# A planner's clock counts TensorE's products by form: a two-layer hybrid trunk on one core

## The chip, the cores and the metric

The kernel runs on one NeuronCore of a Trainium2 chip. The metric is the device time of one execution in microseconds (us), taken as the median over several runs.

## The reference

The program computes a two-layer trunk over 256 context tokens and 256 latent tokens of width 1024, all in float32. Each layer modulates and normalises its tokens, projects them, and runs three mixers side by side (a gated MLP over chunks, a windowed attention with eight heads, a state-space scan), joins them with one output projection, and then applies a feed-forward part. In layer 0 that part is one dense SwiGLU of width 2816 over all 512 tokens. In layer 1 it is a mixture of eight SwiGLU experts of the same width, of which each of the 256 latent tokens takes two:

```
logits = h @ w_r
top_v, top_i = top_k(logits, 2);  gates = softmax(top_v)
out = sum over e of combine[:, e] * ((silu(h @ wg[e]) * (h @ wu[e])) @ wd[e])
x = x + mod[5] * out
```

## The kernel before, in words

**Stages.** Before the experts come the modulation, both mixers and the dense feed-forward (function `phase_a`), then the routing. The experts are the function `experts`. Weights stream from HBM in pieces of 1 MB (two gate-and-up pieces and one down piece for each of the 11 chunks of 256 hidden columns of an expert, so 264 pieces) into a ring of raw buffers `wraw`, which grows to 12 during the experts.

**Places and rounds.** Routed experts are sorted by their number of tokens into eight places with 160, 128, 128, 64, 64, 64, 32 and 32 slots (place 0 is computed as 128 slots and a rest of 32, called NE). Places 0, 1 and 2 are wide: their weights are split into a high part `whi` (ScalarE, L275) and a low part `wlo` (VectorE, L276), each in two halves of 1024 columns, and TensorE makes three fp32r products from the parts, with 512 columns each. Narrow places (64 or 32 slots) use the raw float32 weights with the token block as the stationary operand, two or four products side by side in strips of the array (`tiled`, L1561, for 64 slots and for the down products; `tiled_up`, L1570, for 32 slots). One round of `experts` is one chunk of a wide place (tile `gu`), the down products of the last chunk (`py`), and chunks of narrow places that are dealt out over the rounds; after the narrow up products ScalarE copies them out as `mid`, TensorE turns them (`mTx`, `mT`), and ScalarE and VectorE make the activations `silx`, `mh` and `ml`. A round of place 0 holds its two raw tiles longer, since the rest NE reads them too (`gux`, then `pyx`). The order of places is: four rounds of a 32-slot place alone, 11 rounds of place 1, 11 of place 0, 11 of place 2, two rounds of a 32-slot place alone.

**The planner's clock.** While the program is written out, an object `Order` keeps a clock `clk` in microseconds that stands for TensorE's progress. Every product (`mm`, L368) and every transpose (`tp`, L381) adds a price to it. Side chains (gathering an expert's tokens, `gather`; the transposed one-hot tables, `onehot`; adding an expert's result to the output, `finish`) are generators that yield a delay; `poll` lets a chain take its next step at the next yield of the main program at which `clk` has reached the time that it asked for.

```
f = 1 if (l.dtype == F32R and n >= 256) else 4
self.o.clk += f * max(n, 64) * 0.000422 + 0.002
```

The class `Weights` models the transfers on the same clock: a piece lands at `max(queue + PIECE, clk + LANDS)` (L243), a half split takes `SPLIT` (L277), and a split is laid ahead of its need when `clk` is past the landing and past the last planned split less half a `SPLIT` (`_due`, L288, asked when a product group gives a buffer back). `get` (L311) moves `clk` forward to the planned landing or split of the piece that is needed next.

**What the clock orders.** In the experts TensorE and ScalarE execute in the order in which the program is written (`MSB = "pa"`); VectorE and SyncE, and all engines before the experts (`MSA = ""`), are put in order by the framework's scheduler, for which the written order is the rank. The order of the weight pieces is a fixed list.

Of the kernel before, what the change touches and what calls it, by code (L numbers as in the profile page):

```python
# [10 lines left out]
F32R = mybir.dt.float32r  # L11
# [198 lines left out]
def until(cond):  # L210
    while not cond():
        yield 0.5
# [128 lines left out]
class Net:  # L341
# [26 lines left out]
    def mm(self, out, l, r, start, stop):  # L368
        n = 1
        for x in r.shape[1:]:  # L370
            n *= x
        f = 1 if (l.dtype == F32R and n >= 256) else 4
        self.o.clk += f * max(n, 64) * 0.000422 + 0.002
        self.nc.tensor.matmul(out, l, r, start=start, stop=stop)  # L374

    def warm(self, src, n):
# [2 lines left out]
            self.nc.tensor.matmul(self.idle[:, :256], self.c("ident"), src, start=True, stop=True)  # L379

    def tp(self, out, src, n=P):  # L381
        self.o.clk += 0.11
        ident = self.c("ident")
        self.nc.tensor.transpose(out, src, ident if n == P else ident[0:n, 0:n])  # L384

# [60 lines left out]
    def mods(self, l, ns):  # L446

        ps = self.bulk("modp")
        for i, n in enumerate(ns):
            if l == 0 and 0 < n < 4:  # L450
                self.o.clk += self.SU
                yield
# [1064 lines left out]
        self.ohT[p] = ohT  # L1517

    SU = 4.0
    YB, YH = 1, 1  # L1520
    NRAW, MKRAW = 4, 5
    MPRAW, HL_B, LAG, NS = 3, 2, 6.0, 2
    PIECE, LANDS, SPLIT = 2.45, 4.8, 1.15
    CAPS = (160, 128, 128, 64, 64, 64, 32, 32)
    GROUPS = ((7,), (1,), (3, 4, 5), (0,), (6, NE), (2,))
    AHEAD = {(7, 2): 1, (7, 3): 2, (1, 6): 3, (1, 8): 4, (0, 6): 5}
# [34 lines left out]
    def tiled(self, ps, x, w, ws, a, z):  # L1561

        m = x.shape[-1]
        n = (ws.stop - ws.start) * m // P
        for g in range(P // m):
            self.mm(ps[m * g:m * g + m, :n], x, w[:, ws.start + n * g:ws.start + n * g + n], a, z)
            if g:
                self.o.clk -= 4 * n * 0.000422

    def tiled_up(self, ps, x, w, k):  # L1570

        for g in range(2):
            r = 64 * (k % 2) + 32 * g
            ws = 512 * (k % 4) + 256 * g
            self.mm(ps[r:r + 32, :256], x[:, k, :], w[:, ws:ws + 256], k < 2, k >= KB - 2)
            if g or k % 2:
                self.o.clk -= 4 * 256 * 0.000422

    def narrow_mid(self, ps, m):
        v = self.mp.tile([P, 256], F32, tag=f"mid{m}", name="mid", bufs=2 if m == 32 else 1)  # L1580
# [181 lines left out]
    def finish(self, p):  # L1762

        nc = self.nc
        m = self.slots(p)
        parts = P // m
        w = 512 if m > 32 else 256
        yield from until(lambda: self.ohT.get(p) is not None)
        ohT = self.ohT[p]
        for n in range(2 if m == P else 1):  # L1770
            yh, yl = (self.mp.tile([P, 512], F32R, tag=nm, name=nm, bufs=self.YH) for nm in ("yh", "yl"))
            y = self.mp.tile([P, 512], F32, tag="xsum", name="y", bufs=self.YB)
            if m == P:
                nc.vector.tensor_tensor(y, self.py[p][n], self.mod5row[:, 512 * n:512 * n + 512], op=ALU.mult)
            else:
                for g in range(parts):
                    rows = slice(m * g, m * g + m)
                    nc.vector.tensor_tensor(y[rows, :w], self.py[p][rows, :w], self.mod5row[rows, w * g:w * g + w], op=ALU.mult)  # L1778
            self.split(yh[:, :w], yl[:, :w], y[:, :w])
            yield 3.0  # L1780
            for g in (n,) if m == P else range(parts):
                cs = slice(w * g, w * g + w)
                rows = slice(m * g, m * g + m) if parts > 1 else slice(0, P)
                for t in range(2):
                    pz = self.bank("sc")
                    for i, v in enumerate((yh, yl)):
                        self.mm(pz[:, :w], ohT[rows, t, :], v[rows, :w], i == 0, i == 1)
                    nc.vector.scalar_tensor_tensor(self.acc[:, t, cs], pz[:, :w], self.gate[:, t, p:p + 1], self.acc[:, t, cs],  # L1788
                                                   op0=ALU.mult, op1=ALU.add)
                    if self.ndone == NE:  # L1790
                        nc.sync.dma_start(self.out[P * t:P * t + P, cs], self.acc[:, t, cs])
                    yield 1.0
        del self.ohT[p]
        self.ndone += 1
# [158 lines left out]
```

## Time and profile before

| | |
|---|---|
| Time, median of 3 runs (lowest to highest) | 1577.04 us (1576.43 to 1578.16) |
| The profiled execution: its own time | 1578.03 us |
| The profiled execution: span from first to last instruction | 1576.2 us |
| Mean granted TensorE clock | 0.981 |
| TensorE busy | 1495.8 us (95%) |
| VectorE / ScalarE busy | 820.8 us (52%) / 666.9 us (42%) |
| HBM read | 393.47 MB |

The span begins at 0 us. The dense feed-forward lies between about 350 and 650 us, the first expert piece is multiplied at about 896 us, the rounds of place 0 begin at about 1117 us, the last piece lands at about 1549 us. Windows give busy time of each engine in a stretch, the granted clock (1.00 is 2.4 GHz) and the mean busy share of the 16 DMA engines; "idle" is the engine's time without work, with the instruction that ended it.

### The profile page before, as it was taken

What the parts mean: (1) busy time and instruction counts of PE and PEld (TensorE: products, weight loads), DVE (VectorE), ACT (ScalarE), POOL (GpSimd) and SP (SyncE); (2) the same over time, 40 slices, a digit from 0 to 9 for tenths busy, and PEclk for the clock granted to TensorE, in tenths of its full rate; (3) what the DMA queues carried; (4) which work ended last, traced back from release to release, by engine and by line L of the source; (5) the groups of instructions that cost most, each with busy time, mean ns of one, the idle gap of its engine ahead of it and who ended that gap; (6) DMA issues with size and microseconds to landing.
All of it is one profiled execution on the core that took longest, in us unless ns stands there. A gap on an engine that the chain in (4) does not pass through costs nothing. (4 is left out here: it accounts for less than half of the span.)

```text
span 1576.2 us, 23531 instructions
## 1 busy us (share of the span) xinstructions
PE 1495.8 (95%) x9318; PEld 1077.2 (68%) x9319; DVE 820.8 (52%) x1481; ACT 666.9 (42%) x1189; POOL 102.7 (7%) x135
## 2 busy tenths in 40 slices
PE   4999998899999999999999999999899999999997
PEld 1766675787887787878747776666566666656654
DVE  2687568553333333478775344544465444654545
ACT  3566644343222212356565354444343443433541
POOL 1200123210000000030310000000000000000000
PEclk8999999999999999999999899999999999999998
DMA  9422055432324333234164599999998999999994
GB/s 374 152 107 108 8 211 204 154 133 88 154 81 160 133 107 114 101 135 161 54 260 178 181 406 419 419 419 420 417 397 358 374 410 417 419 408 410 419 420 164
DMA packets 57715, 396.10 MB, mean 251 GB/s; under 512 B 6528, under 2 KB 8576, under 8 KB 10496
## 3 DMA queue, kind: packets, MB, share of 16 engines
q1 hardware_dynamic: 56016, 392.03, 62.5%
q10 hardware_dynamic: 1584, 2.52, 0.5%
q8 instruction: 75, 1.23, 0.3%
q14 instruction: 40, 0.33, 0.1%
HBM read 393.47 MB, written 1.05 MB: 250 GB/s over the span
## 5 line engine op out<-in xcount | busy, mean ns | idle before, releaser
L276 DVE TENSOR_TENSOR wlo<-wraw,whi 128x1024 fp32r<-128x1024 f32 (+2 forms) x318 | 377.0, 1222 | 161.3 <-ACT whi L275 156.0
L275 ACT ACTIVATE whi<-wraw 128x1024 fp32r<-128x1024 f32 (+2 forms) x318 | 320.0, 1047 | 148.4 <-PE fd L374 57.9
L374 PE MATMUL gu<-whi,xw 128*128 128x512 f32 x528 | 167.5, 398 | 4.2 <-ACT whi L275 4.2
L374 PE MATMUL gu<-wraw,xs 128*64 128x256 f32 (+1 forms) x1760 | 168.5, 392 | 0.5 <-ACT xs L1492 0.5
L374 PEld LDWEIGHTS gu<-wraw,xs 128*64 128x64 f32 (+1 forms) x1760 | 95.0, 128 | 65.3 <-issue 16.4
L374 PEld LDWEIGHTS gu<-whi,xw 128*128 128x128 f32 x528 | 95.9, 188 | 24.4 <-ACT whi L275 6.2
L374 PE MATMUL gu<-wlo,xw 128*128 128x512 f32 x264 | 104.3, 395 | 3.5 <-DVE wlo L276 3.5
L1167 DVE TENSOR_TENSOR fsil<-fsil,fu 128x512 f32<-128x512 f32 x22 | 15.1, 688 | 153.5 <-PE fu L374 118.2
L374 PE MATMUL pys<-wraw,silx 128*32 128x256 f32 (+1 forms) x616 | 87.7, 480 | 6.8 <-DVE y L1778 4.1
L430 ACT ACTIVATE fsil<-fg 128x512 f32<-128x512 f32 x22 | 13.1, 598 | 174.3 <-PE fg L374 174.3
L1581 ACT ACTIVATE mid<-gu 128x256 f32<-128x256 f32 x55 | 21.0, 382 | 139.8 <-PE gu L374 139.8
L374 PE MATMUL fg<-ahi,whi 128*128 128x512 f32 (+1 forms) x192 | 72.3, 377 | 0.0
L374 PE MATMUL fg<-alo,whi 128*128 128x512 f32 (+1 forms) x192 | 71.6, 373 | 0.3 <-POOL alo L528 0.3
L374 PE MATMUL fg<-ahi,wlo 128*128 128x512 f32 (+1 forms) x192 | 71.4, 372 | 0.0
L374 PE MATMUL fu<-alo,whi 128*128 128x512 f32 (+1 forms) x192 | 71.4, 372 | 0.0
L374 PE MATMUL fu<-ahi,wlo 128*128 128x512 f32 (+1 forms) x192 | 71.3, 372 | 0.0
L374 PE MATMUL fu<-ahi,whi 128*128 128x512 f32 (+1 forms) x192 | 71.3, 372 | 0.0
L374 PE MATMUL fd<-mhi,whi 128*128 128x512 f32 (+1 forms) x188 | 70.7, 376 | 0.0
L374 PE MATMUL fd<-mhi,wlo 128*128 128x512 f32 (+1 forms) x188 | 70.6, 375 | 0.0
L374 PE MATMUL fd<-mlo,whi 128*128 128x512 f32 (+1 forms) x188 | 70.6, 375 | 0.0
L374 PE MATMUL modp<-wraw,csil 128*32 128x512 f32 x384 | 55.5, 615 | 12.8 <-ACT csil L430 7.4
L374 PEld LDWEIGHTS gu<-wlo,xw 128*128 128x128 f32 x264 | 49.5, 188 | 18.0 <-DVE wlo L276 7.4
(346 smaller groups left out, 2824.8 us busy)
## 6 DMA issues: line engine op xcount, KB each, us to landing
wraw<-in_moe_dram SPq DMA_DIRECT2D x264, 1024.0 KB, 12.6
wraw<-in_wmod_dram SPq DMA_DIRECT2D x48, 1024.0 KB, 6.4
wraw<-in_fgu_dram SPq DMA_DIRECT2D x22, 1024.0 KB, 4.8
wraw<-in_win_dram SPq DMA_DIRECT2D x16, 1024.0 KB, 4.9
wraw<-in_wout_dram SPq DMA_DIRECT2D x8, 1024.0 KB, 6.4
wraw<-in_fdn_dram SPq DMA_DIRECT2D x8, 1024.0 KB, 6.4
wraw<-in_fdn_dram SPq DMA_DIRECT2D x4, 768.0 KB, 4.9
wraw<-in_wgd_dram SPq DMA_DIRECT2D x2, 1056.0 KB, 4.9
```

The lines of the kernel that those rows point to most:

```text
L275: nc.scalar.activation(hi[:, cs], t[:, cs], AF.Copy)
L276: nc.vector.tensor_tensor(lo[:, cs], t[:, cs], hi[:, cs].bitcast(F32), op=ALU.subtract)
L374: self.nc.tensor.matmul(out, l, r, start=start, stop=stop)
L430: self.last_act = self.nc.scalar.activation(out, in_, func, **kw)
L1167: self.nc.vector.tensor_tensor(s, s, pu, op=ALU.mult)
L1581: self.nc.scalar.activation(v, ps[:, :256], AF.Copy)
```

## The change

Products that are fp32r with at least 256 columns cost 0.417 ns a column and 13.5 ns each on the clock; all other products cost four passes of that and 8 ns, at least 0.22 us; a transpose costs 0.19 us instead of 0.11. Products side by side are priced as a group. The two products that add a result to the output get 0.11 us more. The planned time of a piece goes from 2.45 to 2.5 us and that of a half split from 1.15 to 1.2 us. No instruction is added or removed.

```
@@ mm
-        f = 1 if (l.dtype == F32R and n >= 256) else 4
-        self.o.clk += f * max(n, 64) * 0.000422 + 0.002
+        if l.dtype == F32R and n >= 256:
+            self.o.clk += n * self.COL + 0.0135
+        else:
+            self.o.clk += max(0.22, 4 * n * self.COL + 0.008)
@@ tp
-        self.o.clk += 0.11
+        self.o.clk += 0.19
@@ class Net
+    COL = 0.000417
-    PIECE, LANDS, SPLIT = 2.45, 4.8, 1.15
+    PIECE, LANDS, SPLIT = 2.5, 4.8, 1.2
@@ tiled
+        t = self.o.clk + 4 * n * self.COL + (0.033 if n == 256 else 0.1)
         for g in range(P // m):
             self.mm(...)
-            if g:
-                self.o.clk -= 4 * n * 0.000422
+        self.o.clk = t
@@ tiled_up
+        t = self.o.clk + (0.48 if k % 2 else 0)
         for g in range(2):
...
             self.mm(...)
-            if g or k % 2:
-                self.o.clk -= 4 * 256 * 0.000422
+        self.o.clk = t
@@ finish
                     for i, v in enumerate((yh, yl)):
                         self.mm(pz[:, :w], ohT[rows, t, :], v[rows, :w], i == 0, i == 1)
+                    self.o.clk += 0.11
```

## Rows read from the trace of the kernel before

**Rows 1.** Windows by stage: busy time of each engine, granted clock, DMA share, GB/s.

```profile
core 0: us, PE busy (x) PEld busy (x) DVE busy (x) ACT busy (x) POOL busy (x), PEclk, DMA share, GB/s
0.00:350.00 350.00, 313.68 (x1797) 222.91 (x1799) 220.98 (x484) 181.42 (x364) 64.80 (x89) 0.97 0.42 158
350.00:650.00 300.00, 300.00 (x1359) 242.68 (x1358) 98.50 (x131) 72.05 (x92) 0.00 (x0) 1.00 0.33 123
650.00:896.00 246.00, 234.66 (x1537) 187.87 (x1537) 165.16 (x399) 129.11 (x264) 37.92 (x46) 0.98 0.40 152
896.00:1117.00 221.00, 211.70 (x1494) 142.05 (x1492) 95.90 (x134) 99.80 (x174) 0.00 (x0) 0.97 1.00 410
1117.00:1365.00 248.00, 243.52 (x1937) 159.97 (x1938) 126.20 (x178) 105.13 (x174) 0.00 (x0) 1.00 0.97 397
1165.00:1285.00 120.00, 118.84 (x978) 79.71 (x978) 59.18 (x84) 51.98 (x87) 0.00 (x0) 1.00 0.92 374
...
1365.00:1549.00 184.00, 175.70 (x1093) 112.33 (x1093) 99.65 (x130) 76.45 (x117) 0.00 (x0) 0.99 1.01 415
1549.00:1577.00 28.00, 16.52 (x112) 9.40 (x108) 14.40 (x27) 2.89 (x7) 0.00 (x0) 0.76 0.15 49
```

**Rows 2.** The page's GB/s in 40 slices of the span.

```profile
GB/s 374 152 107 108 8 211 204 154 133 88 154 81 160 133 107 114 101 135 161 54 260 178 181 406 419 419 419 420 417 397 358 374 410 417 419 408 410 419 420 164
```

**Rows 3.** Who TensorE waited for, 1117 to 1365 us: total, times, longest.

```profile
PE gu L374 <- ACT whi L275: 2.4, 1, 2.4
PE gu L374 <- DVE wlo L276: 1.0, 2, 0.5
PE sc L374 <- DVE yl L443: 0.7, 1, 0.7
PE sc L374 <- DVE ml L443: 0.7, 1, 0.7
PE mT L384 <- DVE acc L1788: 0.6, 1, 0.6
PE ohT L384 <- DVE oh L1508: 0.4, 1, 0.4
```

**Rows 4.** Timeline, TensorE, the first place-0 rounds: start, length, operation.

```profile
1128.76 1.94 PE L374 MATMUL gux<-wraw,xs 128*32 128x256 f32 x32
1130.51 1.05 PE L374 MATMUL pys<-wraw,silx 128*32 128x256 f32 x16
1131.48 1.95 PE L374 MATMUL gu<-wraw,xs 128*64 128x256 f32 x16
...
1136.57 1.94 PE L374 MATMUL pys<-wraw,silx 128*64 128x512 f32 x8
1138.43 0.66 PE L374 MATMUL mTx<-sel,mid 128*128 128x64 f32 x4
...
1142.95 0.50 PE L374 MATMUL sc<-yh,ohT 128*128 128x512 f32 x1 [0.65 <-DVE ml L443]
...
1149.52 1.93 PE L374 MATMUL gux<-wraw,xs 128*32 128x256 f32 x32
```

**Rows 5.** Chain that ended last, one wide chunk: 24 products of 512 columns.

```profile
1524.06 5.52 PE gu L374 x24
```

**Rows 6.** Who TensorE waited for, 650 to 896 us, the two longest.

```profile
PE S L374 <- ACT prob L430: 3.1, 2, 2.0
PE PTp L384 <- DVE prob L893: 1.8, 3, 0.9
```

**Rows 7.** Windows of 10 us before the experts with a lower granted clock.

```profile
820.00:830.00 10.00, 7.36 (x36) 4.18 (x36) 9.02 (x17) 7.97 (x20) 1.98 (x1) 0.83 0.83 324
250.00:260.00 10.00, 7.44 (x39) 4.61 (x36) 8.11 (x14) 4.96 (x8) 4.27 (x2) 0.85 0.16 39
```

**Rows 8.** Timeline, TensorE, after the last wide place's down products.

```profile
1545.24 1.93 PE L374 MATMUL gu<-wraw,xs 128*32 128x256 f32 x32
1546.99 2.91 PE L374 MATMUL pys<-wraw,silx 128*32 128x256 f32 x24
1549.83 0.50 PE L374 MATMUL sc<-yh,ohT 128*128 128x512 f32 x1
...
1555.75 1.07 PE L374 MATMUL pys<-wraw,silx 128*32 128x256 f32 x16 [0.67 <-DVE silx L1597]
```

**Rows 9.** Timeline, ScalarE, the narrow end of one place-0 round.

```profile
1238.91 1.99 ACT L275 ACTIVATE whi<-wraw 128x1024 fp32r<-128x1024 f32 x2
1242.22 0.38 ACT L1581 ACTIVATE mid<-gu 128x256 f32<-128x256 f32 x1 [1.31 <-PE gu L374]
1245.40 0.38 ACT L442 ACTIVATE mh<-mT 128x256 fp32r<-128x256 f32 x1 [2.80 <-PE mT L384]
```

**Rows 10.** Timeline, TensorE, the same round: the turn that reads that copy.

```profile
1244.76 0.39 PE L384 MATMUL mTx<-const,mid 128*128 128x128 f32 x2
```

## The prediction, made before the change was run

> **What bounds the kernel now.** I read the windows by stage first, then the DMA rate, then the waits of TensorE in the stage that decides. In the dense feed-forward (350 to 650 us) TensorE is busy for all 300.00 us, and order can give nothing there. Before and after it (0 to 350, 650 to 896) TensorE idles 36.3 and 11.3 us, with DMA at 0.42 and 0.40: chains of dependent steps [rows 1]. The experts fall into three parts. From 896 to 1117 the DMA share is 1.00: transfers are the bound, and the 9.3 us in which TensorE idles are paid for by data that has not come. From 1117 to 1365, the rounds of place 0, TensorE is busy for 243.52 of 248.00 us while the DMA share sinks to 0.97: the stretch 1165 to 1285 has 0.92, so (1 - 0.92) x 120 = 9.6 us of transfer time are lost because buffers come back late. TensorE is the bound there, and 4.5 us of idle time is all that order could save. From 1365 to 1549 the share is 0.99 to its end: transfers again. Then comes a tail of 27 us [rows 1]. At 419 GB/s [rows 2] a piece of 1.0486 MB takes 2.50 us, so 264 pieces take 661 us; the experts last 896 to 1549, 653 us, since the first pieces come before 896.
>
> So the end stands where routing ends, plus a stream at a fixed rate, plus what TensorE holds it up in the rounds of place 0, plus the tail. A change of order can touch the first, third and last term alone.
>
> **The prices, checked.** Between two starts of gux lie 20.76 us with one wait of 0.65: 20.11 us of work [rows 4]. It holds 16 strip products for the rest NE, two down calls of a 32-slot place, 8 up calls and two down calls of a 64-slot place, 4 pairs that add results, the turns (two of 64 columns, four transposes) and 36 wide products. Old prices: 1.76 + 0.88 + 3.49 + 1.74 + 1.74 + 0.66 + 7.85 = 18.12 us. New: 1.92 + 0.92 + 3.68 + 2.26 + 1.91 + 1.20 + 8.17 = 20.06. So the new clock is right to 0.05 us in a round, and the old one was 2 us short. The new 2.5 us a piece is the 2.50 of the rows; the old was 2% short as well. On the old clock a place-0 round without a 32-slot chunk (7 pieces, 17.15 us) barely outlasts its transfers; on the new one it outlasts them by 2.5 us (20.06 against 17.50), which is what rows 1 show.
>
> 24 wide products take 5.52 us, 0.230 each [rows 5]; the new price is 0.227, the old 0.218. The Trainium skill, TensorE: Matmul & The Clock Gate, section "Wait — 56ns, not 53.3ns?", has start-to-start times of N/2.4 GHz plus about 2.5 ns, 215.7 ns for 512 columns. By that rule the old price was the right one, the 36 wide products of a round would count 7.77 instead of 8.17 us and the new clock would run 0.4 us ahead per round. The row speaks against it, and I go by the row.
>
> **The change, part by part.** No instruction is added, removed or resized; each edit moves the places at which later steps are written.
>
> 1. *Splits (wide and place-0 rounds).* A split is laid early only when the clock has passed the planned landing. A clock that counts 2 us more per round passes it earlier, so more splits stand ahead of need. The one stall of this kind that counts is at the head of the place-0 rounds: TensorE waits 2.4 us for whi at 1117, and 1.0 us for wlo [rows 3], directly before the stretch in which its time is the bound. Its last product before belongs to the piece just ahead in the list, so the data may have come too late as well. The gain is 0 to 2.4 us for it and 0 to 1.0 for wlo. I take half of the first, 1.2 us. In the two transfer-bound parts, a split laid better saves nothing: the DMA share of 1.00 and 0.99 [rows 1] is the cover. If that cover were gone the 8.3 us idle of 1365 to 1549 would be what is at stake.
>
> 2. *Gathers, one-hots and finishes in the place-0 rounds.* Their delays (1.0, 1.5 and 3.0 us of clock) ran on a clock about 10% slow, so they now end up to 0.3 us of real work earlier, and a finish pair pushes the clock on by 0.56 instead of 0.44. But a chain steps only where the main program yields, one piece of products (about 1 to 5.5 us) apart, so most steps stay where they are. Waits of theirs in this part are two of 0.7 us, one of 0.6 and one of 0.4, 2.4 us in all [rows 3]. (All waits listed there add up to more than the 4.5 us of idle time, since the ends of products are modelled.) I take 0.3 us gained; the bounds are all of it, 2.4 us either way.
>
> 3. *Before the experts.* fp32r products of 512 columns go up 4%, of 256 columns 9% (0.110 to 0.120), a transpose from 0.11 to 0.19; other fp32 products of 128 columns or more stay within 3%. In that stage the written order is only a rank, so a shifted step matters where TensorE has nothing else to do. The longest such place is the end of the second layer's attention, 3.1 us for prob and 1.8 for PTp [rows 6]. I take 0: the steps of a chain that is alone wait for each other in any order. Gain bound: about 3 us of those 4.9. Loss bound: one more wait as long as the longest of them, 2.0, and a stretch such as 820 to 830 us, where after such a wait the granted clock was 0.83 [rows 7]: 17% of 10 us, 1.7 us. Together +4.
>
> 4. *The tail.* The last wide finish is written after its py products with a delay of 3.0. Old clock: 4 x 0.44 for the 32-slot up products, 0.88 for their down products, makes 2.64, under 3.0; the 64-slot down products bring 4.38, and there sc stands, at 1549.83 [rows 8]. New: 1.92 + 0.92 = 2.84, still under 3.0. The next step waits 1.0: old 0.22 + 0.88 = 1.10, new 0.44 + 0.96 = 1.40, both past it after one half of the next up products. Same places, so 0; bounds -1 and +1 us, from the 0.67 us that TensorE waits for silx [rows 8].
>
> 5. *The transfers.* Same order, same sizes. PIECE only tells the planner what the bus does already. 0.
>
> **Sum.** -1.2 - 0.3 + 0 + 0 + 0 = -1.5 us. The profiled execution took 1578.03 us (span 1576.2 and 1.8 around it), so it would be 1576.5; it stands 1.0 above the median of 1577.04, against which I forecast 1575.5. A difference under 0.2%, 3.2 us, is one that a measurement of this kernel can't tell from none.
>
> **The rivals.**
>
> *A, the forecast:* the order improves in a few places, and two stages out of three don't feel it. 1575.5, its own range 1573.9 to 1579. Chance 0.45.
>
> *B, clearly faster:* the place-0 rounds lose all of their 4.5 us of idle time [rows 1], and the attention's end some of its 4.9 [rows 6]. 1577.0 - 4.5 = 1572.5 with the first alone, 1569.5 with 3 us more. For it: the old clock is 10% wrong exactly in the stretch where TensorE is the bound. Against it: in that stretch TensorE is at 98% already. Chance 0.31.
>
> *C, slower before the experts:* a chain's step in the two mixers loses its rank to another, TensorE gets one more wait of about 2 us and then a stretch at a lower granted clock; +4, 1581.0. For it: 250 to 260 and 820 to 830 show 0.85 and 0.83 [rows 7], so the stage lies near the edge. Against it: most of it is busy. Chance 0.12.
>
> *D, slower in the experts:* ScalarE executes as written. If a split is laid ahead of the copy mid of the 64-slot place while its piece has not landed, the copy waits behind it, and the turn on TensorE behind that. Now mid ends at 1242.60 and the turn starts at 1244.76 [rows 9, 10], 2.16 us of cover; a split's two halves take 1.99 [rows 9] and fit. With a wait of one piece (2.5) in front, 2.5 + 1.99 - 2.16 = 2.3 us a round are lost; it decides from the third of the 11 rounds on: 3 x 2.3 = +7, 1584. The Trainium skill, TensorE: Matmul & The Clock Gate, section "Architectural detail", calls ScalarE and VectorE strict FIFO. By that rule a split with late data does hold up every copy behind it. Against D: in these rounds the transfers, not TensorE, wait (share 0.92), so pieces have landed when asked for. Chance 0.08.
>
> *E, nothing:* steps can move only from yield to yield, so the order might stay as it is: 1577.0. Chance 0.04.
>
> **How the numbers follow.** Within 0.2%: A and E, 0.49. Faster: B, 0.31. Slower: C and D, 0.20. The range holds A, E, most of B and half of C: 1570.5 to 1581.5; out of it are D (0.08), the other part of C (0.06) and the far end of B (0.05).
>
> **What would show it.** In the windows of the changed kernel, TensorE's idle time from the head of the place-0 rounds to their end should be 3 us instead of 4.5 and the wait for whi at their head shorter; the lost transfer time should fall by as much, to about 8 us; routing should end at 896 within 2 us; sc should stand after the same products in the tail. A is wrong if routing ends over 3 us earlier or later, if a wait of mid or silx appears in every place-0 round, or if the DMA share falls below 0.98 in the parts that are bound by transfers.

## The result, and the profile after

The changed kernel takes **1599.43 us** (median of 4 runs, 1598.63 to 1601.23) against 1576.95 for the kernel before (4 runs, 1576.43 to 1578.16): a ratio of 1.0143, 95% interval 1.0131 to 1.0156. It is 22.5 us slower, where 1.5 us faster was forecast. The profiled execution has a span of 1596.9 us at a mean granted clock of 0.973 (before: 1576.2 and 0.981).

Nothing was resized, so landmarks tell where the time went. First the kernel before, then the changed one: TensorE's groups of four tiles (fg and fd are the gate and down products of the dense feed-forward), with the least, middle and greatest length in ns and the first and last start.

```profile
L374 PE MATMUL fg<-ahi,whi x192: 279/389/505, 310.1 to 650.0; 128*128 128x512 f32 x160, 128*128 128x256 f32 x32
L374 PE MATMUL fd<-mhi,whi x188: 278/389/390, 415.1 to 685.3; 128*128 128x512 f32 x164, 128*128 128x256 f32 x24
L374 PE MATMUL gu<-wraw,xs x1760: 378/379/637, 895.9 to 1553.2; 128*64 128x256 f32 x118, 128*32 128x256 f32 x78
L374 PE MATMUL gux<-wraw,xs x352: 378/379/404, 1128.8 to 1334.8; 128*32 128x256 f32 x176
```

```profile
L376 PE MATMUL fg<-ahi,whi x192: 277/389/562, 321.5 to 663.2; 128*128 128x512 f32 x160, 128*128 128x256 f32 x32
L376 PE MATMUL fd<-mhi,whi x188: 278/389/389, 428.3 to 698.5; 128*128 128x512 f32 x164, 128*128 128x256 f32 x24
L376 PE MATMUL gu<-wraw,xs x1760: 379/379/636, 913.3 to 1573.6; 128*64 128x256 f32 x118, 128*32 128x256 f32 x78
L376 PE MATMUL gux<-wraw,xs x352: 379/379/403, 1144.9 to 1357.0; 128*32 128x256 f32 x176
```

The dense feed-forward (from 310.1 to 685.3 us in the kernel before, so longer than the 350 to 650 of [rows 1]) begins (first fg) 11.4 us late and ends (last fd) 13.2 late; the experts begin (first gu) 17.4 late; the place-0 rounds begin (first gux) 16.1 late and end 22.2 late, for they last 212.1 instead of 206.0 us; the last gu is 20.4 late. So there are three places: **layer 0's mixers, +11.4; layer 1 and the routing, +4.2; the place-0 rounds, +6.1.** (These three are 21.7; +1.8 in the feed-forward and -1.3 and -1.8 in the other two parts of the experts make the 20.4.)

**Layer 0.** ScalarE's busy time rose by 16 us, though no instruction was added to the program. The groups of its table loads in 200 to 350 us, before and then after (count | busy us, mean ns | idle):

```profile
L430 ACT ACT_TABLE_LOAD x2 | 2.6, 1283 | 0.0
L438 ACT ACT_TABLE_LOAD x1 | 1.3, 1283 | 0.0
```

```profile
L432 ACT ACT_TABLE_LOAD x16 | 20.5, 1283 | 0.4
L440 ACT ACT_TABLE_LOAD x1 | 1.3, 1283 | 0.0
```

Three loads have become seventeen; over the whole execution 28 have become 40, and twelve times 1.283 us is 15.4 of the 16. L438 (L440 after) is the program's own request for a table that holds Ln and Exp together; the others are put in by the compiler ahead of a function (L430, L432) whose table is not there. The Trainium skill, ScalarE: Activation LUTs, section "What ACT_TABLE_LOAD costs", gives some 1283 ns for a load; the rows agree. That section of the Trainium skill adds some 1380 ns of drain to each switch; the rows below show none, for the load at 242.90 begins where z ends and ends where nl begins. The Trainium skill, ScalarE: Activation LUTs, section "Table sets: the hidden batching unit", counts one load for Ln followed by Exp, since one set holds both; here that is so only behind the request. ScalarE's timeline, the kernel before (start, length, operation):

```profile
232.28 0.63 ACT L430 ACTIVATE z<-z 128x512 f32<-128x512 f32 x1
...
234.07 1.28 ACT L438 ACT_TABLE_LOAD   x1
...
245.07 0.21 ACT L430 ACTIVATE nl<-nv 128x8 f32<-128x8 f32 x1 [1.43 <-DVE nv L414]
245.31 0.21 ACT L430 ACTIVATE ne<-nl 128x8 f32<-128x8 f32 x1
```

and the changed kernel:

```profile
241.73 1.15 ACT L432 ACTIVATE z<-z 128x512 f32<-128x512 f32 x2
242.90 1.28 ACT L432 ACT_TABLE_LOAD   x1
244.19 0.21 ACT L432 ACTIVATE nl<-nv 128x8 f32<-128x8 f32 x1
244.42 1.28 ACT L432 ACT_TABLE_LOAD   x1
245.71 0.21 ACT L432 ACTIVATE ne<-nl 128x8 f32<-128x8 f32 x1
```

The function `act_fn` places the request while the program is written: where an Exp or Ln follows another function in the written order, the load is tied behind that function. Before, an Exp (seg) was written between the Silu of z and the Gelus, so a load stood behind z's Silu. With dearer transposes on the clock every seg is written ahead of z, the Gelus follow z's Silu, and the only request is tied behind the last Gelu. The scheduler then runs the Gelus early (219 and 223 us) and z's Silu late (241.73), and from there each Ln and each Exp fetches a table of its own. Who TensorE waited for in 200 to 350 us (total, times, longest), before and after:

```profile
PE gs L374 <- POOL gv L954: 3.9, 2, 2.6
PE ssq L374 <- POOL sq L494: 2.8, 1, 2.8
```

```profile
PE ssq L376 <- POOL sq L496: 5.3, 1, 5.3
PE gs L376 <- POOL gv L956: 4.5, 1, 4.5
```

Windows of 10 us after (columns as in [rows 1]):

```profile
250.00:260.00 10.00, 8.77 (x33) 4.71 (x32) 6.98 (x10) 6.98 (x10) 0.43 (x1) 0.62 0.66 261
260.00:270.00 10.00, 5.46 (x30) 4.18 (x29) 5.91 (x11) 3.83 (x4) 2.59 (x2) 0.72 0.16 61
```

Before, 250 to 260 us had 0.85 [rows 7]. In the next window, too, the clock is now below full; (0.38 + 0.28) x 10 less 0.15 x 10 is at most 5.1 us of TensorE's pace, about half of the 11.4. (Over all windows of 10 us from 200 to 330 us the same sum is 11.9 after and 1.7 before. These are upper figures, since TensorE also waits inside the slow stretches; and the last window, 320 to 330 at 0.71, lies in the feed-forward, which grew by 1.8.)

**Layer 1.** TensorE waits 3.75 us for modrows, before 0.22. ScalarE copies it behind prob, and prob stands behind two table loads round a Gelu. After, TensorE's wait, ScalarE's rows, and a window:

```profile
856.11 1.12 PE L386 MATMUL modt<-const,modrows 128*128 128x128 f32 x4 [3.75 <-ACT modrows L465]
```

```profile
849.52 1.28 ACT L432 ACT_TABLE_LOAD   x1
...
852.64 1.28 ACT L440 ACT_TABLE_LOAD   x1
853.93 0.69 ACT L432 ACTIVATE prob<-S,nm 128x512 f32<-128x512 f32 x1
...
855.46 0.59 ACT L465 ACTIVATE modrows<-modp 128x512 f32<-128x512 f32 x1
```

```profile
850.00:860.00 10.00, 4.94 (x22) 3.57 (x22) 7.56 (x23) 8.36 (x23) 1.15 (x1) 0.75 0.67 259
```

The loads alone are not the difference. The kernel before has the same two (at 831.78 and 834.91), and prob (837.70) and modrows (839.22) stand behind them there too; but TensorE still had products pv to do meanwhile, which in the changed kernel end at 846.9, ahead of both loads. Before, ScalarE and then TensorE:

```profile
834.91 1.28 ACT L438 ACT_TABLE_LOAD   x1
```

```profile
835.45 1.94 PE L374 MATMUL pv<-PT,vtok 128*64 128x256 f32 x14
...
839.87 0.99 PE L384 MATMUL modt<-const,modrows 128*128 128x128 f32 x4 [0.22 <-ACT modrows L463]
```

**Place-0 rounds.** The waits that answer to [rows 3], in 1125 to 1370 us:

```profile
PE sc L376 <- DVE yl L445: 1.8, 1, 1.8
PE sc L376 <- DVE ml L445: 1.6, 2, 0.9
...
PE gu L376 <- ACT whi L275: 0.9, 1, 0.9
```

The wait for whi at the head fell from 2.4 to 0.9, as forecast. But yl and ml rose, and all the loss is at one spot. Windows of 10 us there, before and after (neighbouring rounds have 1.00 in both):

```profile
1178.80:1188.80 10.00, 9.22 (x48) 5.55 (x45) 6.64 (x12) 3.92 (x8) 0.00 (x0) 1.00 1.02 428
1188.80:1198.80 10.00, 10.00 (x86) 6.46 (x88) 4.55 (x8) 3.15 (x5) 0.00 (x0) 1.00 0.57 217
```

```profile
1194.90:1204.90 10.00, 7.27 (x34) 3.77 (x30) 5.84 (x9) 1.88 (x5) 0.00 (x0) 0.74 1.01 425
1204.90:1214.90 10.00, 10.00 (x33) 7.33 (x33) 4.17 (x7) 3.09 (x4) 0.00 (x0) 0.75 0.42 171
```

1.95 us more idle time and (0.26 + 0.25) x 10 = 5.1 us of pace make 7.1, an upper figure (TensorE also waits inside the slow stretch), against the 6.1. The 1.5 won at the head is no part of this: that wait ends before the first gux, in the part that became 1.3 shorter. VectorE's timeline at the spot, before and after:

```profile
1178.05 2.36 DVE L276 TENSOR_TENSOR wlo<-wraw,whi 128x1024 fp32r<-128x1024 f32 x2
1180.33 0.42 DVE L443 TENSOR_TENSOR yl<-y,yh 128x256 fp32r<-128x256 f32 x1
```

```profile
1194.26 3.50 DVE L276 TENSOR_TENSOR wlo<-wraw,whi 128x1024 fp32r<-128x1024 f32 x3
1197.67 0.42 DVE L445 TENSOR_TENSOR yl<-y,yh 128x256 fp32r<-128x256 f32 x1
```

A third half of a split is laid ahead of yl, and TensorE waits 1.8 us for yl, before 0.7 [rows 3].

### The profile page after: what moved, and what is told of

Same layout as the page of the kernel before. It is cut to its first block, busy times and chain, and to the rows that moved or that the text cites. A ratio compares the mean times of both kernels' runs of the same rounds, so it can differ in the third digit from the quotient of the medians.

```text
span 1596.9 us, 23538 instructions
## 1 busy us (share of the span) xinstructions
PE 1504.1 (94%) x9318; PEld 1087.6 (68%) x9319; DVE 818.9 (51%) x1481; ACT 683.2 (43%) x1201; POOL 98.4 (6%) x135
## 5 line engine op out<-in xcount | busy, mean ns | idle before, releaser
L376 PE MATMUL gu<-whi,xw 128*128 128x512 f32 x528 | 171.5, 407 | 3.9 <-ACT whi L275 3.9
L432 ACT ACTIVATE fsil<-fg 128x512 f32<-128x512 f32 x22 | 13.1, 598 | 173.8 <-PE fg L376 173.8
```

Source lines behind the costliest of these rows:

```text
L432: self.last_act = self.nc.scalar.activation(out, in_, func, **kw)
```

## The experiments

Each ratio is against runs of the kernel before in the same job (medians 1577.51 to 1578.91 us, single runs 1572 to 1585).

### Which stage, and which price: e1 to e4

The new prices hold in one stage only, or one of them alone; e1, e3 and e4 have the old ones behind the routing. Shortened, against the kernel before (the set `on` is written out again where a transpose is priced):

```
+        on = set() if self.routed else {'r', 't', 'f'}          # e1
+        on = {'r', 't', 'f', 's', 'z', 'P', 'S'} if self.routed else set()   # e2
+        on = set() if self.routed else {'t'}                    # e3
+        on = set() if self.routed else {'r'}                    # e4
...
-        self.o.clk += 0.11
+        self.o.clk += 0.19 if "t" in on else 0.11
```

(r: fp32r products, f: other products, t: transposes, s: products side by side, z: the finish, P and S: PIECE and SPLIT.)

e1, the new prices until the routing. 

> New prices for products and transposes until routing, all old prices in the experts. Theory 1 (the order before the experts, which the transposes' price shifts, costs most of it): first expert product at 913 us as in the changed kernel, place-0 rounds at their old length of 206 us from first to last gux, total 1577 + 17 = 1594, 1591 to 1597. Rival 2 (the experts' order costs it and the late start is hidden): no more than 1582.

Measured: 1595.75 us, ratio 1.0107 (1.0088 to 1.0127); first fg 321.4, last fd 698.4, first gu 912.6, place-0 rounds 206.1 us. The loss before the experts is whole without any change in the experts.

e2, the new prices behind the routing. 

> Old prices until routing, all new prices in the experts. Theory 1: first expert product at 896 us, place-0 rounds 6 us longer than before, as in the changed kernel, so 1577 + 4 to 6 = 1581 to 1583. Rival 2: 1595 or more. If the experts' new order is harmless by itself and only suffers from the late start: 1577.

Measured: 1583.70 us, 1.0035 (1.0023 to 1.0047); first gu 897.4, place-0 rounds 212.1 us. e1 loses 17.4 us and e2 5.4, together 22.8 against the 22.5 of the whole change, so the two losses add up.

e3, only the transposes' price, until the routing. 

> Only the transpose's price is new, and only until routing (0.19 instead of 0.11). Theory 1: this one number carries the whole delay before the experts, first expert product at 911 to 915 us, total 1591 to 1597. Rival 3 (the fp32r price carries it): 1575 to 1579.

Measured: 1609.54 us, 1.0196 (1.0176 to 1.0216); first fg 322.1, 17 table loads in 200 to 350 us; from the last fd to the first gu 225.2 us instead of 210.6. The direction was right, the size was not: the transposes alone cost layer 0 what all prices cost it, and layer 1 10 us more than those.

e4, only the fp32r price, until the routing. 

> Only the price of fp32r products of 256 and more columns is new, and only until routing. Theory 1: nearly the order of before, first expert product at 896 us within 1, total 1576 to 1578.5. Rival 3: 1590 or more.

Measured: 1578.78 us, 0.9985 (0.9969 to 1.0002); 3 table loads; first gu 892.1 in its profile. No loss. So layer 0's loss comes from the price of a transpose, and layer 1's appears only with it. The price of the other products (f) was not run by itself.

### The table loads: e6 and e7

e6 is the changed kernel with the request put back behind z's Silu; e7 is the kernel before with that request left out (`load_table` not called). Both in layer 0 (y0 is 0).

```
         for z in sz:
             self.act_fn(z[:, self.y0:], z[:, self.y0:], AF.Silu)
+        if self.y0 == 0:
+            self.load_table()          # e6 only
+            self.table = "lnexp"
```

e6: 

> The changed kernel, but in layer 0 the combined table of Ln and Exp is requested behind the Silu of z, where the kernel before requested it. Theory 1 (the 16 extra table loads of 1.28 us, six of them between 242.9 and 262.0 us in the chain from z to the second gv, make the layer-0 delay): table loads in 200 to 350 us fall from 17 to 11 or fewer, the second wait of gs for gv falls from 4.5 us to under 3, the first fg product comes at 311 to 317 us instead of 321.5, and the time is 1587 to 1595 us. Rival 1 (the loads lie beside other work; the delay comes from the places of the steps, the evacuation of gu at 216 instead of 190 us among them): the loads go and the time stays at 1597 to 1601 us.

Measured: 1589.10 us, 1.0062 (1.0038 to 1.0086). Its table loads, the group of fg, and the wait of gs:

```profile
L433 ACT ACT_TABLE_LOAD x6 | 7.7, 1283 | 0.1
L441 ACT ACT_TABLE_LOAD x2 | 2.6, 1283 | 0.0
```

```profile
L377 PE MATMUL fg<-ahi,whi x192: 279/389/504, 311.8 to 651.7; 128*128 128x512 f32 x160, 128*128 128x256 f32 x32
```

```profile
PE gs L377 <- POOL gv L960: 0.5, 1, 0.5
```

And ssq waits 2.8 us for sq, as in the kernel before. Theory 1 holds in each number (though the stage had 14 extra loads, not 16): nine loads fewer give 9.7 of the 11.4 us at the first fg back (11.5 at the last fd) with every price new.

e7: 

> The kernel before, with every price as it was, but the request for the combined table behind the Silu of z in layer 0 is left out. Theory 1: table loads in 200 to 350 us rise from 3 to 12 or more, the first fg product comes at 316 to 323 us instead of 310.1, and the time is 1583 to 1592 us. Rival 1 (the loads cost little where the order is the old one): 1577 to 1580 us.

Measured: 1584.24 us, 1.0037 (1.0019 to 1.0054); 13 table loads, first fg 314.0, last fd 691.1 (before 685.3); op waits 4.9 us for whi, which stands behind the loads on ScalarE, and ssq 5.3 for sq. The time lies in the range of Theory 1, the first fg 2 us under it. The old order, with one request missing, loses about 6 us.

### Layer 1: e10 and e12

```
-        self.o.clk += 0.11
+        self.o.clk += 0.19 if not self.routed and getattr(self, 'l', 0) == 1 else 0.11   # e10, e12
...
-        self.nc.scalar.activation(rows, ps, AF.Copy)
+        if l == 1:                                                            # e12
+            self.nc.vector.tensor_copy(rows, ps)
+        else:
+            self.nc.scalar.activation(rows, ps, AF.Copy)
```

e10: 

> The new prices until the routing, except that a transpose costs the clock 0.11 us in layer 0 and 0.19 us from the first projection of layer 1 on; the old prices in the experts. Theory 3 (each layer loses by its own order of steps; layer 1 lost 3.5 us in the changed kernel and 14.6 us with the transposes' price alone): the first fg product at 309 to 311 us as before, the stretch from the last fd to the first gu 213 to 226 us instead of 210.6, and the time is 1580 to 1592 us. Rival 3 (layer 1 loses only because layer 0 ends late, and so its weights come at other times): 1576 to 1579.5 us.

Measured: 1581.90 us, 1.0019 (1.0006 to 1.0032); first fg 307.8, from the last fd to the first gu 215.7 us; modt waits 3.7 us for modrows. Layer 1 loses by an order of its own, not because layer 0 is late. Its size is uncertain: in nine kernels with the old transposes' price before the experts (before, e2, e7, e8, e11, e14 to e17) the stretch takes 210.6 to 213.2 us; in the seven with the new price in layer 1 (changed, e1, e3, e6, e10, e12, e13) it takes 214.2 to 225.2.

e12: 

> The kernel with the transposes' new price in layer 1 alone (1581.9 us), in which VectorE instead of ScalarE copies modrows in layer 1. Theory 3 (modt's wait of 3.7 us for modrows, a copy that stands on ScalarE behind prob and a table load, and the low clock behind it cost the stretch its 5 us): that wait falls under 1.5 us, the stretch from the last fd to the first gu falls from 215.7 to 210 to 213 us and the time is 1576 to 1580 us. Rival 3 (the copy only makes VectorE late, or the S products behind prob hold the stretch anyway): 214 us or more and 1581 to 1585 us.

Measured: 1581.39 us, 1.0016 (1.0000 to 1.0032); the stretch lasts 214.4 us. The wait got shorter and not enough: modt waits 2.2 us for modrows, and PTp now 2.5 for prob, in e10 0.9. Rival 3 of that run stands: other waits take its place. What makes layer 1 late was not found in one instruction, and stays open.

### The place-0 rounds: e8, e11, e14 to e17

e8, e11, e16 and e17 start from e2, e14 and e15 from the kernel before.

```
-            yield 3.0
+            yield 5.0                                         # e8
...
-            self.split(yh[:, :w], yl[:, :w], y[:, :w])        # e11, e14
+            nc.scalar.activation(yh[:, :w], y[:, :w], AF.Copy)
+            nc.gpsimd.tensor_tensor(yl[:, :w], y[:, :w], yh[:, :w].bitcast(F32), op=ALU.subtract)
...
+                    self.o.clk += 0.11                        # e15: this new price alone, in finish
...
         self.routed = True
+        self.SPLIT = 1.4                                      # e16
+        self.PIECE, self.SPLIT = 2.7, 1.15                    # e17
```

e8: 

> The kernel with all new prices behind the routing alone (which took 1583.7 us), with 5.0 instead of 3.0 us between the piece of y and its two sc products in a finish. Theory 2 (the 6 us of the place-0 rounds are lost at one finish near 1180 us, where VectorE makes three wlo halves ahead of yl, sc waits 1.8 us for it, and TensorE's granted clock halves behind that wait): the sc products stand further back, the wait falls under 0.5 us, the place-0 rounds last 205 to 208 us and the time is 1576.5 to 1579.5 us. Rival 2 (the delay only moves the sc products behind products that wait for the same VectorE queue): 210 us or more and 1582 to 1586 us.

Measured: 1589.22 us, 1.0068 (1.0043 to 1.0094); place-0 rounds 213.3 us. The wait for yl is gone, but ml is now waited for 2.9 us in all and py 1.3 for wlo; the clock is 0.88 and 0.78 in 1160 to 1180. Rival 2's side in the rounds, and slower than it said. (Its profile's span is 6.3 us longer than e2's: 0.8 up to the first gu, where nothing was edited, 1.2 in the place-0 rounds and 4.5 behind them, less 0.2 between. So most of it is not lost in these rounds.)

e11: 

> The kernel with the new prices behind the routing alone (1583.7 us), in which a finish computes yl on GpSimd instead of VectorE; the order of TensorE's instructions stays what it was in that kernel. Theory 2 (VectorE's third wlo half ahead of yl is what costs the place-0 rounds 6 us): sc waits under 0.5 us for yl, TensorE keeps its full clock through these rounds, they last 205 to 208 us and the time is 1576 to 1579.5 us. Rival 2 (the order of TensorE itself is at fault, or the ml behind it): 210 us or more and 1581 to 1586 us.

Measured: 1580.81 us, 1.0016 (1.0004 to 1.0028); place-0 rounds 209.6 us. Between the two: the wait for yl is gone and 2.5 us with it, but two others grew behind VectorE's halves, and the clock falls behind the one for ml.

```profile
PE sc L377 <- DVE ml L446: 2.5, 2, 1.6
PE mT L387 <- DVE acc L1794: 1.7, 2, 1.0
```

e14: 

> The kernel before, with yl on GpSimd. sc waits 0.7 us for yl in the place-0 rounds of the kernel before. If that wait is all that yl costs there: 1576 to 1579 us, no difference that can be measured. If the wait behind VectorE's wlo halves costs more than it shows: 1573 to 1576 us.

Measured: 1579.15 us, 1.0009 (0.9998 to 1.0019): no difference that can be measured.

e15: 

> The kernel before with one new price alone: 0.11 us more for the two sc products of a finish. It leaves TensorE's order as it was but for three places, and lays the third wlo half ahead of the first yl on VectorE, as all new prices together do. Theory 2 (the place of that one half makes the 6 us of the place-0 rounds): sc waits 1.5 us or more for yl, TensorE's granted clock falls under 0.8 in the 20 us behind it, the place-0 rounds last 210 to 213 us instead of 206 and the time is 1581 to 1585 us. Rival 2 (the rest of the new order is needed for the loss): 205 to 208 us and 1576 to 1579 us.

Measured: 1579.71 us, 1.0005 (0.9995 to 1.0015); place-0 rounds 206.9 us. Its wait and its window:

```profile
1182.41 0.38 PE L377 MATMUL sc<-yl,ohT 32*128 32x256 f32 x1 [1.79 <-DVE yl L446]
```

```profile
1179.20:1189.20 10.00, 8.21 (x46) 4.88 (x41) 6.10 (x10) 2.29 (x6) 0.00 (x0) 1.00 1.01 425
```

The third half ahead of yl makes the whole wait of 1.8 us and costs only 1: the clock stays at 1.00. Theory 2 falls in its size. The comparison with e2 is close, for TensorE has the same instructions in both from 1170 to 1183 us, within 0.06 us of each other, the wait of 1.79 among them. Yet the next instruction, eight products of a down call, takes 1.94 us in e15 and 2.46 in e2; first e15, then e2:

```profile
1182.72 1.94 PE L377 MATMUL pys<-wraw,silx 128*64 128x512 f32 x8
```

```profile
1182.76 2.46 PE L377 MATMUL pys<-wraw,silx 128*64 128x512 f32 x8
...
1188.77 0.58 PE L377 MATMUL sc<-yh,ohT 32*128 32x256 f32 x1 [0.93 <-DVE ml L446]
```

and windows of 2 us behind it, e15 and e2:

```profile
1184.00:1186.00 2.00, 2.00 (x15) 1.27 (x12) 0.49 (x2) 0.00 (x0) 0.00 (x0) 1.00 1.01 426
```

```profile
1184.00:1186.00 2.00, 2.00 (x7) 0.63 (x3) 0.07 (x2) 0.00 (x0) 0.00 (x0) 0.51 1.00 422
```

In e2 the clock falls to its lower level, 1.2 GHz, behind the first wait; the wait for ml comes later and lies in the slow stretch already. In the changed kernel and in e6 it falls at the same spot.

e16: 

> The kernel with all new prices behind the routing alone (1583.7 us), in which a split of half a piece costs the clock 1.4 instead of 1.2 us behind the routing; the first yl then stands ahead of all three wlo halves. Theory 2: sc does not wait for yl, full clock, place-0 rounds of 203 to 206 us and 1575 to 1578 us, if the halves that are laid later do not make the products of the next expert late. Rival 2: the products wait for wlo or whi instead, 209 us or more and 1580 to 1586 us.

Measured: 1582.04 us, 1.0018 (1.0004 to 1.0033); place-0 rounds 212.6 us. The stall has moved forward, to waits of 0.64 us for rest at 1153.06 and 1.17 for yl at 1154.70; the clock is 0.75 in 1149.30 to 1159.30 us and 0.73 in the next 10. Rival 2 stands in its time, by another stall than it named.

e17: 

> The same kernel with 2.7 instead of 2.5 us for a transfer and 1.15 for a split behind the routing, which lays two wlo halves ahead of the first yl again, as in the kernel before, with the other new prices kept. Theory 2: place-0 rounds of 204 to 207 us at the full clock, 1576 to 1579 us. Rival 2: 209 us or more and 1580 to 1585 us.

Measured: 1597.45 us, 1.0119 (1.0100 to 1.0137). The place-0 rounds last 207.2 us at the full clock, with the waits for ml still at 1.6: that much of Theory 2 is right. The time is not: the transfer-bound parts became longer, from the first gu to the first gux 245.6 instead of e2's 231.9 us, from the last gux to the last gu 230.3 instead of 216.3. There TensorE's waits for whi and wlo rose from 8.0 to 13.5 and from 0.2 to 6.2 us, and the clock fell from 0.98 to 0.95 and 0.96; that 2.7 us for a transfer that takes 2.5 lays splits late fits the waits, and was not shown further. (The profile is of its slowest execution, 1604.44 us.)

The four orders side by side, by the length of the place-0 rounds: neither the third half nor the rest of the new order, 206.0 us (before); the half alone, 206.9 (e15); the rest without the half (and with other prices of transfer and split), 207.2 (e17); both, 212.1 (e2). Each is from one profile, but the lengths repeat: 212.1 in the changed kernel and e6 too, 206.1 in e1, e3, e4, e7, e10 and e12. Each alone costs about 1 us. Together they cost 6, of which up to 5 are pace: the clock falls behind the wait for yl. Why it falls there in e2 and not in e15, behind the same work and the same wait, no row shows; it stays open.

### All remedies: e13

The edits of e6, e11 and e12 on the changed kernel. 

> The changed kernel with the three remedies together: the request for the combined table behind the Silu of z in layer 0, yl on GpSimd, modrows of layer 1 copied by VectorE. If the three stalls make the whole loss (10 us for the tables, which the run with the request alone showed, 6 us for yl, 3 to 5 us for modrows): 1575 to 1582 us, no more than 0.3% from the kernel before. If the changed order costs something in many small places: 1583 to 1589 us.

Measured: 1587.48 us, 1.0060 (1.0039 to 1.0082). It is the second case: the first fg comes at 313.4, the last fd at 690.0, the stretch to the first gu lasts 215.9 and the place-0 rounds 209.6 us. Beyond the table loads the new order costs something in several places, and mending the longest wait uncovers the next. No version was found that beats the kernel before by more than its interval; e4 comes nearest.

## Why the prediction was wrong

**Step 3 failed.** It put the stage before the experts at 0, where e1 loses 17.4 us, because there "the written order is only a rank" and "the steps of a chain that is alone wait for each other in any order". The rank is not all that the written order sets: `act_fn` decides by it where a table is requested. e6 and e7 show that price, 9.7 us and about 6. The loss bound of +4 was built from the longest wait and the lowest clock that the kernel before already had, so it could not hold an instruction that ran three times there and seventeen times after. The sentence on transposes (0.11 to 0.19, 73% more) was written and not followed up; e3 shows that this price alone makes layer 0's loss, e4 that the fp32r price makes none. The prediction's own sign, routing over 3 us late, came up: the first gu is 17.4 late.

**Rival C** had the place and the kind (a lost step, one wait, a lower clock), at +4 and 0.12. Layer 1 is such a case by its size, +4.2, and +5.1 in e10, of which up to 2.6 can be scatter. Its mechanism stays open beyond the rows: modrows behind two table loads and prob, as before, and nothing left for TensorE to do meanwhile.

**Step 1** was right on the head of the place-0 rounds (2.4 to 0.9 us, forecast -1.2; the half of 2.4 was chosen, not worked out) and wrong to count it alone. Nor does a run show that the shorter wait gave time: e15 keeps the 2.4, and its part from the first gu to the first gux takes 230.5 us, after the change 231.6. A split laid earlier also stands earlier in VectorE's queue; this kernel's yl and ml stand in that queue. Nothing that was queued behind a split was named there.

**Rival D** named the right kind of harm, a split ahead of another step, on the wrong engine: no wait for mid or the turn stands among those of the place-0 rounds. On VectorE it came about: yl stood behind three halves for 3.4 us. The Trainium skill, TensorE: Matmul & The Clock Gate, section "Architectural detail", calls both engines strict FIFO; the trace agrees for VectorE: yh, the copy that yl needs, ended at 1194.68, and yl began at 1197.67, behind the third half.

**Step 2** bounded its waits at 2.4 us either way; those for yl and ml rose by 2.0 in all, inside it. What it left out is the clock: up to 5.1 us of pace behind 2 us of waits. It had the row for it, 0.83 after a wait [rows 7], but used it before the experts only.

**Steps 4 and 5** held. In the tail, sc still follows the 64-slot down products, and the transfers lost most where TensorE held them up (386 GB/s over the same 248 us from the head of the place-0 rounds, 397 before [rows 1]; 411 and 410 ahead of them, 405 and 415 behind). PIECE is not neutral in general, though: at 2.7 us (e17) the kernel is some 14 us slower than e2. The check of the prices held too, but a clock that fits the trace did not give a faster order: correcting the transposes' price alone cost most of all (e3).

## What to carry to other kernels

Where a program decides things by its written order (a table request, a tie between two instructions), a change of cost estimates can change what is executed and not only when; list those decisions, and count the executed instructions of each kind in the stage after the change. On a TensorE that is 95% busy, price a new wait at both ends, with the clock kept (here 1 us) and with the clock lost behind it (6 us). When a planner's costs are made truer, expect the new order to be another order and not a better one, and time it price by price.

## What the runs showed of the hardware that was not expected

An Ln and an Exp that follow each other each get a table load of 1.28 us of their own when nothing has requested the common one: six loads between 242.90 and 263.25 us in the changed kernel, one in that place in the kernel before. And the same 13 us of products with the same wait of 1.79 us ended at the full clock in e15 and at half of it in e2, so what a wait costs could not be read from the wait.
